# A feature-major residual stream, a second FFN input buffer and a new order of work in a streaming encoder layer on eight cores

## Chip, cores and metric

The kernel runs on the 8 cores of one Trainium2 chip (two dies: cores 0 to 3 and 4 to 7). All cores run the same program, each on its own two prompt sequences (eight tiles of 512 frames) and one sample of 64 frames. The time is the span of the slowest core in microseconds (us). Some executions fall into a slow state, in which a whole die shows a lower granted TensorE clock: of the 12 runs of the changed kernel with cores on record, 8 kept a mean clock of at least 0.96 on every core, and in the other four one die or both showed 0.80 to 0.92. Engines have the profile's names: PE is TensorE, DVE VectorE, ACT ScalarE, POOL GpSimd, SP SyncE. PSUM (tiles named `ps`) holds the sums that PE writes, and L773 is line 773 of that kernel's source.

## The reference

One layer, in JAX, cut to what matters:

```
h = x + 0.5 * swiglu(rms_norm(x, norm_ffn1), w_ffn1_in, w_ffn1_out)          # FFN1
n = rms_norm(h, norm_mix)
q_a,k_a,v_a,r_a,f_a, q_b,k_b,v_b, g_a,g_b = split(n @ w_in)
o_a, s_new = gla_branch(...)         # gated scan, 4 heads, a state passed from chunk to chunk
o_b        = band_attention(...)     # 16 heads, own chunk and the 8 before, learned bias
mixed = sigmoid(g_a) * (o_a @ w_branch_gla) + sigmoid(g_b) * (o_b @ w_branch_att)
h = h + mixed @ w_out                                                        # the "mixer" ends
h = h + 0.5 * swiglu(rms_norm(h, norm_ffn2), w_ffn2_in, w_ffn2_out)          # FFN2
y = rms_norm(h, norm_final)          # d_model 1024, d_ff 2816; keys, values and state are outputs too
```

## The kernel before

The program is a list of operations with priorities, which a scheduler in Python turns into a fixed order per engine. Two streams are woven into each other: F (the FFNs) and M (the mixer: projections, gated scan, attention, merge). In tile i's period, M works on tile i, while F does FFN2 of tile i-1 and FFN1 of tile i+1. FFN matmuls are what TensorE (PE) does while the scan or the attention waits for other engines; I call them filler below.

```
groups = [[tiles[0], make_sample()]] + [[t] for t in tiles[1:]]
P.seg = (-1, "F")
for c in groups[0]: prelude(c)            # load x, norm, transposes into xF
ffn1(0, groups[0])
for i in range(NTILE):
    P.seg = (i, "F")
    if i > 0:
        ffn(i - 1, groups[i - 1], 2)
    if i + 1 < NTILE:
        for c in groups[i + 1]: prelude(c)
        ffn1(i + 1, groups[i + 1])
    P.seg = (i, "M")
    mixer_with_state(i, groups, tiles, mixer)
```

Within a period both streams advance in proportion to their `pace`, which is the PE time of an operation except for attention's score product:

```
P.pe(0.3, qk, r=[qb] + [...], w=[sc], pace=2.2)
```

Weights arrive as fp32. In its first uses a block is cast to bf16 by the load itself, from the POOL queue; then it is stored as bf16, and later uses load that from the SP queue:

```
def wload(cls, blk, i):                   # i: how often the block has been used
    b = P.buf(cls, 4096, "w")
    first = blk % 3
    if i <= first:
        P.load(... in_=wsrc[blk] ..., q="pool")           # fp32 to bf16, 128 x 2048
        if i == first:
            P.store(... out=wsc[blk] ..., q="sp")
    else:
        P.load(... in_=wsc[blk] ...)                      # bf16
```

The residual stream has tokens on the partitions, so each norm sums along the row (DVE, with an accumulator) and transposes the result on PE.

The softmax here doesn't subtract the row's maximum and nothing guards it: scores larger than these inputs give would overflow.

Of the kernel before, what the change touches and what calls it, by code (L numbers as in the profile page):

```python
# [30 lines left out]
    "hF": (5 * 4096, 4096), "hM": (2 * 4096, 4096), "xF": (8192, 8192), "xM": (8192, 8192),  # L31
    "gT": (22 * 1024, 1024), "F": (9 * 1024, 1024), "M": (38 * 1024, 256), "Sb": (8 * 512, 512), "st": (64 * 16, 16),
# [34 lines left out]
class Op:  # L67
    __slots__ = ("eng", "dur", "fn", "deps", "bufs", "wbufs", "dma", "idx", "prio", "seg", "pace", "start", "end", "nwait",
                 "out", "ready", "seq", "sig", "waits", "vc", "dsem", "dval", "sval", "bytes", "nd")


class Program:
# [12 lines left out]
    def op(self, eng, dur, fn, r=(), w=(), dma=False, nbytes=0, pace=None):  # L85
# [38 lines left out]
        o.sig = False  # L124
# [7 lines left out]
    def act(self, n, fn, r=(), w=()):  # L132
        return self.op("act", 0.2 + n * 0.00084, fn, r, w)

    def dve(self, n, fn, r=(), w=()):
        return self.op("dve", 0.11 + n * 0.00105, fn, r, w)

    def pool(self, n, fn, r=(), w=()):
        return self.op("pool", 0.15 + n * 0.0018, fn, r, w)

    def load(self, fn, nbytes, r=(), w=(), q="sp", dur=0.06):
        return self.op(q, dur, fn, r, w, dma=True, nbytes=nbytes)

    def store(self, fn, nbytes, r=(), w=(), q="pool", dur=0.9):
        return self.op(q, dur, fn, r, w, dma=True, nbytes=2 * nbytes)

    def schedule(self, lead):
# [10 lines left out]
        for o in ops:  # L158
            o.out = []
            o.ready = 0.0  # L160
            o.nd = 0
        for o in ops:
            for d, _ in o.deps:
                ops[d].out.append(o.idx)
                o.nd += 1
# [14 lines left out]
        for o in ops:  # L180
            if o.nd == 0:
                avail[o.eng].append((o.prio, o.idx))
        efree = {e: 0.0 for e in ENGINES}
# [3 lines left out]
        ev = [0.0]  # L187
        done = 0
# [38 lines left out]
        while done < nops:  # L227
# [13 lines left out]
            while ev and ev[0] <= tnow + 1e-9:  # L241
                heapq.heappop(ev)
            progress = True
            while progress:
                progress = False
                for e in ENGINES:
# [3 lines left out]
                    for item in avail[e]:  # L250
                        if best is not None and item >= best[0]:
                            continue
                        o = ops[item[1]]
                        if o.ready > tnow + 1e-9:
                            continue
                        spots = []
                        ok = True
                        for b in o.bufs:
                            if id(b) not in placed:
                                p = find(b, tnow)  # L260
                                if p is None:
                                    ok = False
                                    break
                                spots.append((b, p))
# [8 lines left out]
                        best = (item, o, spots)  # L273
                    if best is None:
                        continue
                    item, o, spots = best
                    avail[e].remove(item)
                    for b, p in spots:
# [10 lines left out]
                        unal[b.cls].remove(b)  # L289
                    o.start = tnow  # L290
                    if o.dma:
                        efree[e] = tnow + o.dur
                        s0 = max(tnow + o.dur, bw_free)
                        x = o.bytes / 300e3
                        bw_free = s0 + x
                        o.end = s0 + x + 2.2
# [12 lines left out]
                    for b in o.bufs:  # L309
                        b.users.append(o)  # L310
                        b.left -= 1
                        if b.left == 0:
# [15 lines left out]
                            heapq.heappush(ev, ft)  # L328
                    for d in o.out:
# [6 lines left out]
                        if x.nd == 0:  # L336
                            avail[x.eng].append((x.prio, x.idx))
# [123 lines left out]
def mmt(ncols, n):  # L461
    return n * (max(ncols, 240) * 0.000417 + 0.003)
# [13 lines left out]
]  # L476
LEAD = {"M": 0.04, "F": 0.0}


def build(NSEQ, SEQLEN):  # L480
# [14 lines left out]
    xp = din("xp", [NTOK, D])  # L495
    xsm = din("xs", [64, D])
# [6 lines left out]
    gains_d = din("gains", [128, 4, 8])  # L503
    gnf_d = din("gnf", [1, D])
# [4 lines left out]
    yp = dout("yp", [NTOK, D])  # L509
    ys = dout("ys", [64, D])  # L510
    kpo = dout("kpo", [NSEQ * 512, D])
    vpo = dout("vpo", [NSEQ * 512, D])
    spo = dout("spo", [NSEQ, 4, 128, 256])
    kso = dout("kso", [64, D])
# [4 lines left out]
    h1d = dscr("h1d", [NTOK + 64, D], F32)  # L519
    h2d = dscr("h2d", [NTOK + 64, D], F32)  # L520
# [19 lines left out]
    gains = sb("gains", [128, 4, 8], F32)  # L540
    gnfb = sb("gnfb", [128, D], F32)
# [5 lines left out]
    CMASK = constf[:, 1, :]  # L547

    out_dmas = []
    K = {n: Buf(None, 0, n, base=n) for n in ("kbT", "VB", "Sf", "ident", "constf", "segm", "gains", "gnf", "eps", "cbs",  # L550
# [5 lines left out]
    def init():  # L556
# [3 lines left out]
        P.dve(128, lambda e: e.tensor_copy(out=identb[:], in_=constf[:, 0, :]), r=[K["constf"]], w=[K["ident"]])  # L560
        P.dve(1, lambda e: e.memset(epsb[:], EPS), w=[K["eps"]])

    def init2():
        P.seg = (-0.5, "M")
        P.load(lambda e: e.dma_start(out=wfa[:], in_=wfa_d), 64 << 10, w=[K["wfa"]], q="pool", dur=0.9)
        P.load(lambda e: e.dma_start(out=wgate[0:17, :], in_=wgate_d), 32 << 10, w=[K["wgate"]], q="pool", dur=0.9)
        P.load(lambda e: e.dma_start(out=gnfb[:], in_=gnf_d.partition_broadcast(128)), 512 << 10, w=[K["gnf"]])
# [24 lines left out]
    def wload(cls, blk, i):  # L592
        b = P.buf(cls, 4096, "w")
        first = blk % 3
        if i <= first:
            P.load(lambda e: e.dma_start(out=b.b(), in_=wsrc[blk]), 1 << 20, w=[b], q="pool", dur=0.9)
# [11 lines left out]

    def norm_stat(hb, TP, cls):
        xb = P.buf(cls, 2048, "xb")  # L610
        st = P.buf("st", 16, "st")
        P.dve(1024, lambda e: e.scalar_tensor_tensor(out=xb.b()[:TP, :], in0=hb.f()[:TP, :], scalar=1.0, in1=hb.f()[:TP, :],  # L612
                                                     op0=MUL, op1=MUL, accum_out=st.f()[:TP, 0:1]), r=[hb], w=[xb, st])
        rstd(st, TP, 0, 1, 1.0 / D)
        return xb, st

    def norm_sub(ctx, s, hb, gidx, xdst, strm):
        TP = ctx.TP
        xb, st = norm_stat(hb, TP, strm)
        P.dve(600, lambda e: e.tensor_scalar(out=xb.b()[:TP, :], in0=hb.f()[:TP, :], scalar1=st.f()[:TP, 0:1], scalar2=None,  # L620
                                             op0=MUL), r=[hb, st, xb], w=[xb])
        pb = P.buf("ps" + strm, 2048, "tp")

        def tr(e):
            ins = None
            for k in range(8):
                ins = e.transpose(out=pb.b()[:, k * 128:k * 128 + TP], in_=xb.b()[:TP, k * 128:(k + 1) * 128],
                                  identity=identb[:TP, :TP])
            return ins
        P.pe(0.9, tr, r=[xb, K["ident"]], w=[pb])  # L630

        def ev(e):
            src = pb.b().rearrange("p (k t) -> p k t", k=8)[:, :, 0:TP]
            dst = xdst.b().rearrange("p (k t) -> p k t", k=8)[:, :, s * 128:s * 128 + TP]
            g3 = gains[:, gidx, :].unsqueeze(2).broadcast_to([128, 8, TP])
            return e.tensor_tensor(out=dst, in0=src, in1=g3, op=MUL)  # L636
        P.dve(8 * TP, ev, r=[pb, K["gains"]], w=[(xdst, s)])

    def xk(x, ctx):
        return [(x, s) for s in range(ctx.NS)]  # L640

    def xcols(x, k, ctx):
        return x.b().rearrange("p (k t) -> p k t", k=8)[:, k, 0:ctx.T]

    def xsub(x, k, s, ctx):
        return x.b().rearrange("p (k t) -> p k t", k=8)[:, k, s * 128:s * 128 + ctx.TP]
# [3 lines left out]

    def proj(w, c0, ncol, outs, keys):
        def fn(e):
            ins = None
            for k in range(8):
                for o, x, ctx in outs:
                    ins = e.matmul(o(), lhsT=w3(w, k, c0, ncol), rhs=x(k), start=(k == 0), stop=(k == 7))
            return ins
        dur = sum(mmt(ctx.T, 8) for _, _, ctx in outs)
        return P.pe(dur, fn, r=[w] + keys, w=[])
# [6 lines left out]
    def prelude(ctx):  # L666
        ctx.xF = P.buf("xF" if ctx.NS == 4 else "F", ctx.T * 16, "xF")
        for s in range(ctx.NS):
            pre_sub(ctx, s)

    def pre_sub(ctx, s):
        hb = P.buf("hF", 4096, "h")
        TP = ctx.TP
        P.load(lambda e: e.dma_start(out=hb.f()[:TP, :], in_=ctx.x(s)), TP << 12, w=[hb])
        norm_sub(ctx, s, hb, 0, ctx.xF, "F")

    def ffn(i, ctxs, which):
        wi, wo_ = (W_F1I, W_F1O) if which == 1 else (W_F2I, W_F2O)
        c0 = ctxs[0]
        cs = ctxs[1] if len(ctxs) > 1 else None  # L680
        for c in ctxs:
            c.gT = []
            if c.NS == 1:
                c.gTs = P.buf("F", NJ * 128, "gTs")
        for j in range(NJ):
            ffn_j(i, ctxs, c0, cs, wi + j, j)
        blocks = {}
        for half in range(2):
            acc = {}
            for c in ctxs:  # L690
                for s in range(c.NS):
                    acc[(c, s)] = P.buf("psF" if c is c0 else "psM", 2048, "acc")
            j = 0
            while j < NJ:
                u = half * NJ + j
                n = min(4 - u % 4, NJ - j)
                if u // 4 not in blocks:
                    blocks[u // 4] = wload("ringF", wo_ + u // 4, i)
                for c in ctxs:
                    for s in range(c.NS):  # L700
                        ffn_o(c, s, acc[(c, s)], blocks[u // 4], j, n, u % 4)
                j += n
            for c in ctxs:
                for s in range(c.NS):
                    ffn_e(c, s, acc[(c, s)], half, which)
# [853 lines left out]
```

## Time and profile before

| kernel before | |
|---|---|
| median, all runs of the first session | 4124.12 us (4116.39 to 4605.45) |
| profiled run (fast) | span 4114.9 us |
| PE busy, mean granted clock | 89 %, 0.954 to 0.956 |

### The profile page before, as it was taken

How to read it: one execution, taken by the hardware profiler on the slowest of the kernel's cores; microseconds unless marked ns; L12 is line 12 of the kernel's file. 1: busy time of each engine (PE TensorE's matmuls, PEld its weight loads, DVE VectorE, ACT ScalarE, POOL GpSimd, SP SyncE). 2: the span in 40 equal slices, each digit the busy share in tenths (PEclk: the TensorE clock that was granted, in tenths of full speed). 3: DMA queues.
4: the chain of work that ended last, by engine and by line, in shares of the span. 5: the costliest groups of instructions: out<-in, count | busy, mean ns of one | idle time of the engine just before them, and what ended most of it. 6: DMA issues, size and time to landing. Idle time of an engine off the chain costs nothing.

```text
span 4114.9 us, 60621 instructions; the slowest of 8 cores (4098.3 to 4114.9 us)
## 1 busy us (share of the span) xinstructions
PE 3659.6 (89%) x19384; PEld 1692.0 (41%) x19760; DVE 1755.8 (43%) x2918; ACT 1759.3 (43%) x3324; POOL 392.7 (10%) x795
## 2 busy tenths in 40 slices
PE   3789977897989989999899979999999989999787
PEld 1334433443434434444444434443444434444333
DVE  3245333525435353453425453453425453453333
ACT  2325443524535445254543535254533546254432
POOL 2011111110021101010010000000010000001100
PEclk8999989998999989999899989999999999999799
DMA  9687857775688745755446444634445444644243
GB/s 208 123 185 165 169 121 174 146 155 166 177 217 203 176 166 166 223 171 174 154 146 215 141 160 151 220 132 151 147 153 206 141 159 141 209 150 154 88 153 123
DMA packets 200374, 677.12 MB, mean 165 GB/s; under 512 B 30575, under 2 KB 31232, under 8 KB 200064
## 3 DMA queue, kind: packets, MB, share of 16 engines
q1 hardware_dynamic: 141248, 492.52, 35.7%
q0 software_dynamic: 58816, 180.69, 22.1%
q8 instruction: 166, 2.72, 0.3%
q14 instruction: 144, 1.18, 0.1%
HBM read 668.72 MB, written 121.37 MB: 192 GB/s over the span
## 4 chain that ended last, share of the span: by engine, by line
PE 78%; DVE 6%; issue 5%; ACT 5%; DMA 4%; POOL 0%; ACTq 0%; DVEq 0%; SPq 0%; POOLq 0%
PE ps L726 27%; PE ps L754 14%; PE ps L799 8%; PE ps L1010 6%; PE ps L1228 5%; PE ps L1234 5%; PE ps L1116 3%; PE ps L844 2%; PE ps L1083 2%; PE ps L1260 2%; DMA s_ringM<-w 1%; DMA s_hM<-h1d 1%; ACT s_M L1098 1%; DMA s_ringF<-w 1%; DVE s_F L612 1%
## 5 line engine op out<-in xcount | busy, mean ns | idle before, releaser
L726 PE MATMUL ps<-s_xF,s_ringF 128*128 128x512 bf16 x5466 | 1312.9, 382 | 74.3 <-DVE s_F L740 40.9
L726 PEld LDWEIGHTS ps<-s_xF,s_ringF 128*128 128x128 bf16 x5632 | 538.2, 98 | 743.2 <-issue 166.0
L754 PE MATMUL ps<-s_ringF,s_gT 128*128 128x512 bf16 x2739 | 649.0, 380 | 7.2 <-issue 3.6
L740 DVE TENSOR_TENSOR s_F<-ps,s_F 128x512 f32<-128x512 f32 (+1 forms) x396 | 252.7, 638 | 600.9 <-ACT s_F L664 560.7
L662 ACT ACTIVATE s_F<-ps 128x512 f32<-128x512 f32 (+1 forms) x396 | 219.5, 554 | 650.2 <-PE ps L726 568.6
L1098 ACT ACTIVATE s_M<-ps 128x1024 bf16<-128x1024 f32 (+1 forms) x288 | 286.8, 997 | 411.0 <-DVE ps L1091 362.9
L754 PEld LDWEIGHTS ps<-s_ringF,s_gT 128*128 128x128 bf16 x2816 | 264.0, 98 | 324.8 <-issue 35.8
L799 PE MATMUL ps<-s_ringM,s_xM 128*128 128x512 bf16 x1503 | 351.9, 387 | 13.6 <-DVE s_xM L636 4.8
L1091 DVE TENSOR_TENSOR ps<-ps,s_bias 128x512 f32<-128x512 f32 (+1 forms) x304 | 182.0, 599 | 280.8 <-PE ps L1083 274.5
L1010 PE MATMUL ps<-s_xM,s_ringM 128*128 128x512 bf16 x1001 | 254.5, 405 | 30.9 <-ACT s_M L1098 22.4
L604 ACT ACTIVATE s_st<-s_st,s_epsb 128x1 f32<-128x1 f32 (+2 forms) x168 | 49.2, 293 | 535.6 <-DVE s_F L612 283.4
L741 DVE TENSOR_TENSOR s_gT<-ps,s_F 128x512 bf16<-128x512 f32 x352 | 242.5, 689 | 66.4 <-PE ps L726 45.6
L1243 DVE TENSOR_TENSOR s_M<-ps,s_M 128x512 f32<-128x512 f32 (+1 forms) x144 | 92.0, 639 | 418.0 <-PE ps L1234 233.5
L1228 PE MATMUL ps<-s_xM,s_ringM 128*128 128x512 bf16 x1000 | 242.6, 383 | 16.6 <-ACT s_M L663 9.3
L1234 PE MATMUL ps<-s_M,s_ringM 128*128 128x512 bf16 (+1 forms) x1129 | 246.4, 359 | 3.7 <-DVE s_M L1243 2.3
L663 ACT ACTIVATE s_F<-s_F 128x512 f32<-128x512 f32 (+1 forms) x396 | 232.5, 587 | 28.8 <-ACT s_F L662 0.4
L664 ACT ACTIVATE s_F<-s_F 128x512 f32<-128x512 f32 (+1 forms) x396 | 232.3, 587 | 28.6 <-ACT s_F L663 2.2
L662 ACT ACTIVATE s_M<-ps 128x512 f32<-128x512 f32 (+2 forms) x210 | 118.3, 563 | 284.2 <-PE ps L1228 258.8
L799 PEld LDWEIGHTS ps<-s_ringM,s_xM 128*128 128x128 bf16 x1536 | 148.3, 99 | 194.9 <-issue 35.0
L1116 PE MATMUL ps<-s_M,s_VB 128*128 128x256 bf16 (+3 forms) x888 | 185.7, 324 | 12.0 <-POOL s_M L1104 7.7
L1083 PE MATMUL ps<-s_M,s_kbT 64*128 64x256 bf16 (+3 forms) x896 | 117.3, 317 | 59.0 <-ACT s_M L1098 24.0
L1010 PEld LDWEIGHTS ps<-s_xM,s_ringM 128*128 128x128 bf16 x1024 | 101.3, 103 | 152.7 <-issue 60.9
(150 smaller groups left out, 3587.3 us busy)
## 6 DMA issues: line engine op xcount, KB each, us to landing
s_ringF<-wsc SPq DMA_DIRECT2D x396, 512.0 KB, 3.6
s_ringM<-wsc SPq DMA_DIRECT2D x265, 512.0 KB, 4.1
s_ringF<-w POOLq DMA_DIRECT2D x132, 512.0 KB, 7.0
s_ringM<-w POOLq DMA_DIRECT2D x87, 512.0 KB, 8.0
wsc<-s_ringF SPq DMA_DIRECT2D x66, 512.0 KB, 5.5
s_hF<-xp SPq DMA_DIRECT2D x64, 512.0 KB, 5.4
wsc<-s_ringM SPq DMA_DIRECT2D x44, 512.0 KB, 6.1
s_bias<-btd SPq DMA_DIRECT2D x64, 256.0 KB, 3.0
```

The source lines that it names most:

```text
L662: P.act(n, lambda e: e.activation(out=s.f()[:TP, 0:n], in_=src(), func=AF.Exp, scale=-1.0), r=r, w=[s])
L663: P.act(n, lambda e: e.activation(out=s.f()[:TP, 0:n], in_=s.f()[:TP, 0:n], func=AF.Ln, bias=1.0), r=[s], w=[s])
L726: ins = e.matmul(o(), lhsT=w3(w, k, col, 128), rhs=x(k), start=(k == 0), stop=(k == 7))
L740: P.dve(n, lambda e: e.tensor_tensor(out=s.f()[:, 0:n], in0=g(), in1=s.f()[:, 0:n], op=MUL), r=r1 + [s], w=[s])
L741: P.dve(n, lambda e: e.tensor_tensor(out=gt.b()[:, gk * 64:gk * 64 + n], in0=u(), in1=s.f()[:, 0:n], op=MUL), r=r2 + [s], w=[(gt, gk)])
L754: ins = e.matmul(acc.f()[:TP, :], lhsT=c.gT[j + jj][0].b()[:, c.gT[j + jj][1] * 64 + s * 128:c.gT[j + jj][1] * 64 + s * 128 + TP], rhs=w.b ...
L799: ins = e.matmul(pb.f()[:c.TP, :], lhsT=xsub(x, k, s, c), rhs=ws[k // 4].b()[:, (k % 4) * 512:(k % 4 + 1) * 512], start=(k == 0), stop=(k ...
L1010: ins = e.matmul(pb.f()[:, 0:T], lhsT=w3(w, k, col, 128), rhs=xcols(c.xM, k, c), start=(k == 0), stop=(k == 7))
L1098: return e.activation(out=b, in_=a, func=AF.Exp, scale=0.125)
L1116: ins = e.matmul(acc[hh]()[:, s0 * 128:(s0 + ns) * 128], lhsT=vl(slot(j), 2 * pr + hh), rhs=pp.b()[:, hh * 512 + col:hh * 512 + col + ns * ...
L1228: ins = e.matmul(pg.f()[:, 0:T], lhsT=w3(w, k, 0, 128), rhs=xcols(c.xM, k, c), start=(k == 0), stop=(k == 7))
L1234: ins = e.matmul(px.f()[:, 0:T], lhsT=w3(w, k, 128, 128), rhs=src[k].b()[:, 0:T], start=(k == 0), stop=(k == 7))
```

## The change

Its intent: no norm transposes and fewer other PE operations; FFN work always at hand for the tiles in the middle; an earlier start. The core of the diff (cuts marked):

```
-    "hF": (5 * 4096, 4096), "hM": (2 * 4096, 4096), "xF": (8192, 8192), ...
+    "xF": (2 * 8192, 8192), ...                          # F and M pools grow, hF and hM go
-    xp = din("xp", [NTOK, D])
+    xp = din("xp", [NTILE, 8, 128, 512])                 # features on partitions; so yp, h1d, h2d
...
     def wload(cls, blk, i):
-        first = blk % 3
+        first = blk % 3 if blk >= W_QKB else 1 + blk % 2 # FFN blocks: cast twice or three times
...
+    class Norm:                                          # in place of norm_stat, norm_sub
+        def add(self, h):      # ACT: Square of one chunk; POOL (the last: DVE): add to the sum
+        def rstd(self):        # PE: fp32 all-ones product over the 128 partitions; ACT: Ln, Exp
+    def scaled(...)            # DVE: x * gain * rstd, once per chunk
...
-        for half in range(2): ...                        # FFN out: tokens stationary, 4 sums at once
+        for m in range(8): ffn_m(...)                    # FFN out: weights stationary, 1 sum of 22
-            P.pe(mmt(128, 8 * c.NS), fn, ...)            # separate product for the key output: gone
...
-        P.pe(0.3, qk, ..., pace=2.2)
+        P.pe(0.35, qk, ..., pace=8.0 if c.i in (0, NTILE - 1) else 2.2)
...
+    ffn_in(0, groups[0], 1)                              # prologue: PSUM and weight slots of M borrowed
+    for c in groups[1]: prelude(c)
+    ffn_out(0, groups[0], 1)
     for i in range(NTILE):
         P.seg = (i, "F")
-        if i > 0: ffn(i - 1, groups[i - 1], 2)
-        if i + 1 < NTILE: prelude(...); ffn1(i + 1, ...)
+        if i > 0: ffn_in(i - 1, groups[i - 1], 2)
+        if 0 < i < NTILE - 1: prelude(groups[i + 1])     # before FFN2's output product
+        if i > 0: ffn_out(i - 1, groups[i - 1], 2)
+        if i + 1 < NTILE: ffn_in(i + 1, ..., 1); ffn_out(i + 1, ..., 1)
```

## The prediction

> **What bounds the kernel now.** I read the page first (engine totals, slices), then two windows, then the PE timeline inside them, then the chain of waits of the first 100 us.
>
> ```profile
> PE 3659.6 (89%) x19384; PEld 1692.0 (41%) x19760; DVE 1755.8 (43%) x2918; ACT 1759.3 (43%) x3324; POOL 392.7 (10%) x795
> PE   3789977897989989999899979999999989999787
> PEclk8999989998999989999899989999999999999799
> DMA  9687857775688745755446444634445444644243
> ```
>
> (Page: busy us, share and instructions; then tenths of each fortieth of the span.) PE is the bound; every other engine is under half busy. But PE dips in the first three slices, in slices 6 and 7, in the last three and once per tile, and the granted clock dips with it. The two windows show a dip beside a dense stretch:
>
> ```profile
> 930.00:985.00 55.00, 31.21 (x149) 13.03 (x151) 35.75 (x50) 18.28 (x35) 5.49 (x14) 0.66 0.58 177
> 1000.00:1200.00 200.00, 198.55 (x977) 88.38 (x996) 68.30 (x107) 103.64 (x155) 27.47 (x54) 1.00 0.73 184
> ```
>
> (Second number: length; then PE busy.) In the dense stretch PE is busy 198.55 of 200 us at clock 1.00; in the dip 31 of 55 at 0.66. The timeline says why:
>
> ```profile
> 973.92 1.01 PE L627 MATMUL ps<-s_identb,s_F 128*128 128x128 bf16 x8 [1.23 <-DVE s_F L620]
> 979.39 1.01 PE L627 MATMUL ps<-s_identb,s_F 128*128 128x128 bf16 x8 [3.07 <-DVE s_F L620]
> ...
> 1043.72 0.39 PE L1083 MATMUL ps<-s_M,s_kbT 64*128 64x512 bf16 x2
> 1044.04 3.63 PE L726 MATMUL ps<-s_xF,s_ringF 128*128 128x512 bf16 x16
> ```
>
> L1083 is an attention score product, which must be followed by bias, exp and mask elsewhere. Dense stretches fill that wait with 3.6 us of FFN matmuls (L726). In the dip the FFN stream has nothing: FFN2 has ended, and the next tile's norm and transposes (L627) must write the one input buffer before FFN1 can start. Attention stands bare. The FFN stream is without matmuls from 936 to 985, 1456 to 1494, 1946 to 1978, 2410 to 2443, 2863 to 2902 and 3330 to 3368 us. The start is a different fault:
>
> ```profile
> 21.23 42.90 DMA s_ringM<-w
> 64.67 22.41 DMA s_ringF<-w
> ```
>
> [...]mixer weights, caches and bias stores stand ahead of the FFN's fifth weight block, so PE waits until 87.7 us.
>
> [...]16 attention projections at N=512 take 3.45 us at 1034.3 in the chain, so 216 ns[...]8 such matmuls take 3.44 us at 550.4, double[...]
>
> **The floor and the loss.** I counted every matmul in each built program[...] the 512 and 64 wide ones, 216 and 29 ns in the timeline[...]. Before: 19,760 matmuls, 14,776 of them 512 wide, sum 3524 us. Span 4115, so 591 us are lost. Cut at the first forget-gate product (L813) of each tile, which start at 258, 698, 1233, 1722, 2211, 2660, 3128 and 3592 us, the nine stages last 258, 439, 536, 489, 490, 449, 467, 464, 523 against floors of 139, 337, 451, 441, 447, 412, 431, 431, 434. Lost: 119, 102, 85, 48, 42, 37, 36, 33, 89.
>
> **The change part by part.**
>
> ```profile
> L627 PE MATMUL ps<-s_identb,s_F 128*128 128x128 bf16 (+1 forms) x528 | 49.6, 252 | 104.4 <-DVE s_F L620 103.8 <-DVE s_gT L741 0.4
> L1034 PE MATMUL ps<-s_ringM,s_xM 128*128 128x128 bf16 x512 | 31.2, 219 | 0.0
> L612 DVE SCALAR_TENSOR_TENSOR s_F<-s_hF 128x1024 bf16<-128x1024 f32 (+1 forms) x99 | 119.6, 1220 | 16.8 <-DMA s_hF<-xp 14.6
> L663 ACT ACTIVATE s_F<-s_F 128x512 f32<-128x512 f32 (+1 forms) x396 | 232.5, 587 | 28.8 <-ACT s_F L662 0.4
> L1217 POOL TENSOR_TENSOR s_M<-s_M 128x512 bf16<-128x512 f32 x72 | 83.4, 1158 | 617.6 <-DVE s_M L1243 617.5
> ```
>
> (Busy, mean ns, idle before.) 1. The residual stream lies feature-major. All 792 norm transposes go: 768 x 56 + 24 x 29 ns = 44 us of floor. The key output reuses the projection (L1034 goes): 512 x 56 + 64 x 56 = 32 us. FFN-out and out-projection swap operands: the same 512-wide count for prompts; the sample's 104 wide matmuls become 416 narrow: -22 + 12 = -10 us. Added: 36 FP32 all-ones products for the norm sums, 32 x 4 x 216 ns + 4 small = 28 us. Net -58 us: the built program gives 3466. By stages: 137, 324, 453, 435, 430, 412, 430, 430, 417.
>
> 2. Other engines. DVE loses the statistics, scaling and transposed evictions (L612 160 us in both streams, its accumulator reads 11, L620 74, L636 117, L781 42: 404) and gains 256 scalings and 50 adds of about 0.67 us plus small ones, some 215: near 1570. ACT gains 256 squares at 0.587 and 64 Ln/Exp at 0.587 (188, with the sample 197) and loses 132 rstd pairs at 0.293 + 0.202 (65): near 1890. POOL gains 174 adds at 1.16 and 24 small ones (208) and some 150 DMA issues at 0.53 (80): near 680. At 3690 us these are 43, 51 and 18%: none becomes the bound, so this is all off the path except in norm tails.
>
> 3. Order. A second FFN input buffer, and the prelude of the next tile placed before FFN2's output product. In the new PE order FFN-in follows FFN-out directly and every score product of the middle tiles has FFN work behind it. So the FFN stream's gap closes: in the 55 us window above, PE was idle 24. I count 24 in each of six tiles, 144 us.
>
> 4. Residual tiles out of the general buffers instead of two. Now out-projection waits for a store to free its buffer, then a load: at 1679 the chain has 9.0 + 6.0 us of DMA. I count some 12 us (one such wait, part of it covered) at each of six tile boundaries, 72 us.
>
> 5. Start: PSUM and weight slots of the idle mixer stream are borrowed, caches come later, 16 weight blocks stand together at the head of POOL's queue, FFN1 blocks aren't stored in tile 0. First FFN matmul: x at about 18 us as now (transposes start at 18.2), then square, add, FP32 product, Ln, Exp and paced scalings, some 6 + 4: 28 us lost. Then 22 blocks at 3.9 us (now 6 us each from 100 to 195 us, one in flight). I allow 10 for DMA and 7 for the tail: loss 45 instead of 119.
>
> 6. First and last tile: attention's pace is raised from 2.2 to 8, so FFN work is spread under it. Losses 102 to 35 and 89 to 55 (bare attention at 3800-3900 goes; the last FFN2's 16 us tail and 10 us head stay). For the tiles between, parts 3 and 4 make 216 us of 85 + 196; I book 201, since gap and boundary partly overlap: the second tile, which keeps three PSUM banks per step while the sample runs (waits of 1.8 us on L740 at 743), goes from 85 to 35, the other five from 196 to 45.
>
> Sum: 3466 + 45 + 35 + 35 + 45 + 55 = 3681; I say 3690.
>
> **Rivals.** A: DMA takes over early. Cast loads rise from 219 to 252. The queue table gives queue 1 492.5 MB in 35.7% of the span, 335 GB/s, so 1.56 us for a bf16 block; queue 0 has 22.1%, 909 us, of which its 65 MB of stores take 195 at that rate, and 219 cast blocks the other 714: 3.26 us each. Estimate: the first 175 us need 33 cast FFN blocks, some 6 for the mixer and 13 MB besides, 127 + 39 = 166 us; tile 0, some 360 us long, needs 69 cast blocks (225), 31 block stores (49) and 17 MB (51), 325 us. For it: share 0.85 already now over 0 to 258 us. Against: it reaches 1.1 to 1.2 under backlog between 25 and 100 us. It would add 40 to 80: 3730 to 3770. B: the norm's chain (ACT, POOL, PE, ACT, DVE) becomes the new wait at tile ends. Against: the order puts 5 to 12 us of FFN matmuls behind each of its products. If they don't cover it, 8 us (six steps of 0.6 to 0.9 and the paced scalings) at 16 ends, 128 us: 3810. C: only the floor moves, because bare attention is bound by its own exp chain: 4115 - 58 = 4057. Against: the dense stretches at clock 1.00 with the same attention.[...]
>
> **Range and chances.** The floor is firm to 10 us; the loss of 215 could be 150 (all dips closed) or 330 (A or B): 3616 to 3796, so 3620 to 3800. Faster by over 2% needs under 4042[...]. 0.96 / 0.03 / 0.01.
>
> **What would show it.** Mean clock near 0.98, PE busy near 95%, the per-tile dips gone from the slices, first FFN matmul by 30 us and first forget-gate product near 180; ACT near 1890, DVE near 1570, POOL near 680. FP32 products near 0.9 us each. Wrong if early slices keep 7s with PE waiting on weight DMA (A), if PE's waits name the norm's DVE scalings (B), or if dips stay with FFN matmuls available (C).

## More of the kernel before

For what follows I cut the span into nine stages, at the first forget-gate product (512 columns) of each tile. The stage before tile 0 is the start; the last one holds tile 7's mixer and its FFN2. Three of these stages of the kernel before, as windows (from:to, length, then busy us and count of PE, weight load, DVE, ACT and POOL, granted clock, DMA share, GB/s):

```profile
258.00:698.00 440.00, 370.59 (x2321) 179.07 (x2363) 191.22 (x370) 190.74 (x438) 67.26 (x122) 0.93 0.74 157
2660.00:3128.00 468.00, 442.52 (x2197) 200.97 (x2239) 210.88 (x337) 213.27 (x382) 29.05 (x68) 0.97 0.47 160
3592.00:4115.00 523.00, 457.95 (x2345) 208.43 (x2388) 202.27 (x322) 215.93 (x376) 39.89 (x84) 0.93 0.41 136
```

PE stands still for 69, 25 and 65 us in these three. The first and the last stage are the poor ones, and only one FFN call runs beside the mixer in each.

## The result, and the profile after

| | before | after |
|---|---|---|
| median of all runs | 4129.20 us (17 runs) | 3865.28 us (11 runs) |
| lowest run | 4116.39 us | 3854.78 us |
| ratio of fast runs | | 0.9368 (95 % interval 0.9353 to 0.9382) |

A ratio is the mean time of one kernel's fast runs over that of the other's fast runs of the same rounds, so it is not quite the ratio of these medians. Executions in which one die ran at a lower clock are left out of the means. The direction was right and the time was not: 3690 us and a range of 3620 to 3800 us were predicted.

The page of the changed kernel (fast run, span 3866.4 us): engine totals, then fortieths of the span in tenths.

```profile
PE 3589.8 (93%) x18776; PEld 1619.7 (42%) x18776; DVE 1595.9 (41%) x2784; ACT 1903.3 (49%) x3420; POOL 696.7 (18%) x1143
PE   5878888989989999999999999999999999988988
PEclk9988999999999999999999999999999999989999
DMA  7896699777898956777474555545464545533454
```

The middle of the span is now solid nines. What is left are the lower digits at the left (all of slices 1 to 7, two more up to slice 12) and at the right (four of the last five), just where the kernel before was poor as well. The stages as windows:

```profile
0.00:219.00 219.00, 149.23 (x1090) 73.45 (x1090) 84.60 (x190) 80.67 (x186) 49.39 (x96) 0.95 0.82 161
219.00:652.00 433.00, 367.61 (x2254) 171.38 (x2253) 160.45 (x332) 199.27 (x439) 101.88 (x171) 0.92 0.79 161
2481.00:2915.00 434.00, 431.98 (x2149) 193.88 (x2148) 189.61 (x313) 231.66 (x390) 65.61 (x104) 1.00 0.52 173
3349.00:3866.00 517.00, 446.77 (x2090) 192.34 (x2090) 188.93 (x309) 228.75 (x378) 67.15 (x114) 0.93 0.41 140
```

In the third, a middle tile, PE is busy 432 of 434 us at a granted clock of 1.00. In tile 0 (second) and the last stage (fourth) it still stands 65 and 70 us, and the clock is lower there (0.92 and 0.93). DMA is busy in tile 0 (0.79) and calm in the last stage (0.41), so the two need not have the same cause.

Cut in the same way on all eight cores, with the median of the cores in each stage (us). The floor is an estimate, the prediction's count of matmuls, and "predicted" its floor plus its loss. The time for each matmul agrees with the spacing of starts in the trace of the kernel before: 216 ns at 512 columns (16 take 3.45 us at 1034.3), 56 ns at 128 (32 of L1034 from 1852.99 us) and 29 ns at 64 (16 of L1010 from 445.45 us).

| stage | before | floor | predicted | after | after minus predicted |
|---|---|---|---|---|---|
| start | 257 | 137 | 182 | 209 | +27 |
| tile 0 | 436 | 324 | 359 | 431 | +72 |
| tile 1 | 537 | 453 | 488 | 509 | +21 |
| tiles 2 to 6 | 2354 | 2137 | 2182 | 2181 | -1 |
| tile 7 and end | 522 | 417 | 472 | 516 | +44 |

The median core takes 3842 us; the slowest, which sets the time, 24 us more in the profiled run. So the sum over the middle tiles is right to a microsecond, and the whole miss lies in the first three stages and the last. The agreement of that sum is in part luck: the prediction spread 45 us of loss over five tiles, and they lost 15, 13, 7, 4 and 5.

### The profile page after: what moved, and what is told of

Same layout as the page of the kernel before. It is cut to its first block, busy times and chain, and to the rows that moved or that the text cites. A ratio compares the mean times of both kernels' runs of the same rounds, so it can differ in the third digit from the quotient of the medians.

```text
span 3866.4 us, 60436 instructions; the slowest of 8 cores (3822.3 to 3866.4 us)
## 1 busy us (share of the span) xinstructions
PE 3589.8 (93%) x18776; PEld 1619.7 (42%) x18776; DVE 1595.9 (41%) x2784; ACT 1903.3 (49%) x3420; POOL 696.7 (18%) x1143
## 3 DMA queue, kind: packets, MB, share of 16 engines
q0 software_dynamic: 65632, 198.00, 26.2%
## 4 chain that ended last, share of the span: by engine, by line
PE 79%; DMA 9%; DVE 4%; ACT 4%; issue 3%; POOL 1%; SPq 0%; DVEq 0%; ACTq 0%; POOLq 0%
PE ps L773 28%; PE ps L803 14%; PE ps L831 8%; PE ps L1042 5%; PE ps L1249 5%; PE ps L1255 5%; PE ps L876 3%; PE ps L1137 3%; PE ps L1291 2%; DMA s_ringM<-w 2%; PE ps L1104 2%; DMA s_M<-xs 1%; DMA s_F<-xp 1%; ACT s_M L1119 1%; DMA s_ringF<-w 1%
## 5 line engine op out<-in xcount | busy, mean ns | idle before, releaser
L773 PE MATMUL ps<-s_xF,s_ringF 128*128 128x512 bf16 x5456 | 1298.9, 384 | 34.7 <-DVE s_xF L661 15.5
L773 PEld LDWEIGHTS ps<-s_xF,s_ringF 128*128 128x128 bf16 x5456 | 521.9, 99 | 674.1 <-issue 124.3
L803 PE MATMUL ps<-s_gT,s_ringF 128*128 128x512 bf16 x2736 | 643.2, 381 | 8.3 <-DMA s_ringF<-w 5.0
L1119 ACT ACTIVATE s_M<-ps 128x1024 bf16<-128x1024 f32 (+1 forms) x288 | 286.4, 994 | 310.1 <-DVE ps L1112 276.3
L803 PEld LDWEIGHTS ps<-s_gT,s_ringF 128*128 128x128 bf16 x2736 | 262.4, 98 | 333.7 <-issue 38.7
L640 ACT ACTIVATE s_F<-s_F 128x512 f32<-128x512 f32 x192 | 119.0, 627 | 282.6 <-DVE s_F L817 217.7
L1249 PE MATMUL ps<-s_xM,s_ringM 128*128 128x512 bf16 x1024 | 243.5, 381 | 4.8 <-DVE s_M L1090 2.1
L1042 PE MATMUL ps<-s_xM,s_ringM 128*128 128x512 bf16 x1024 | 235.3, 381 | 8.2 <-ACT s_M L1119 6.8
L646 POOL TENSOR_TENSOR s_F<-s_F 128x512 f32<-128x512 f32 x126 | 160.0, 1270 | 323.8 <-ACT s_F L640 308.3
L1137 PE MATMUL ps<-s_M,s_VB 128*128 128x256 bf16 (+3 forms) x896 | 173.7, 306 | 7.8 <-POOL s_M L1125 4.5
L817 DVE SCALAR_TENSOR_TENSOR s_F<-ps,s_F 128x512 f32<-128x512 f32 x128 | 87.8, 689 | 173.5 <-PE ps L803 142.8
```

Of the source, the lines that this page charges most:

```text
L773: ins = e.matmul(o(), lhsT=w3(w, k, col, 128), rhs=x(k), start=(k == 0), stop=(k == 7))
L803: ins = e.matmul(acc[c].f()[:, 0:c.T], lhsT=w.b()[:, (u + jj - j) * 128:(u + jj - j + 1) * 128], rhs=g.b()[:, k * 64:k * 64 + c.T], start= ...
L1042: ins = e.matmul(pb.f()[:, 0:T], lhsT=w3(w, k, col, 128), rhs=xcols(c.xM, k, c), start=(k == 0), stop=(k == 7))
L1119: return e.activation(out=b, in_=a, func=AF.Exp, scale=0.125)
L1137: ins = e.matmul(acc[hh]()[:, s0 * 128:(s0 + ns) * 128], lhsT=vl(slot(j), 2 * pr + hh), rhs=pp.b()[:, hh * 512 + col:hh * 512 + col + ns * ...
L1249: ins = e.matmul(pg.f()[:, 0:T], lhsT=w3(w, k, 0, 128), rhs=xcols(c.xM, k, c), start=(k == 0), stop=(k == 7))
```

## The experiments

Theories after the result. Theory A (rival A of the prediction): early casting loads and stores of weights hold the start, tile 0 and tile 1. Theory F (of filler): filler is a fixed stock. Beside tile 0's mixer there is only FFN1 of tile 1, beside tile 7's only FFN2 of tile 6, so raising attention's pace merely takes filler from the scan. Unless said otherwise, each run is the changed kernel with one edit, results are correct, the numbers are means of fast runs (the changed kernel: 3864.3 us), and stages are medians of the eight cores in one profiled run. A ratio stands for the time over that of the kernel before, with its 95 % interval; the changed kernel has 0.9368. Python lays out the order of work anew for each edit, so an edit can also move other operations.

### 1. The pace put back

```
-  pace=8.0 if c.i in (0, NTILE - 1) else 2.2
+  pace=2.2
```

> The changed kernel with the pace of attention in the first and last tile put back from 8 to 2.2, nothing else. Theory F (filler is a fixed stock: in these two tiles only one FFN call runs beside the mixer, so spreading it only decides whether the gated scan or the attention stands bare): time within 1 % of the changed kernel, 3827 to 3904 us, loss of the last stage still 85 to 110 us, but the scan dense and the attention bare. Rival P (the prediction's step: the pace is what covers attention): the last stage and tile 0 lose 60 to 100 us more, 3930 to 3970 us.

Measured: 3863.5 us (ratio 0.9374, 0.9345 to 0.9403): the same. Tile 0 took 445 us rather than 431, the last stage 512 rather than 516. What PE waited for in the mixer of the last tile (wait, total us, times, longest), the changed kernel and then this one:

```profile
PE ps L1104 <- ACT s_M L1119: 16.9, 15, 2.4
PE ps L1009 <- POOL s_Sb L999: 8.8, 10, 1.5
```

```profile
PE ps L1104 <- ACT s_M L1119: 22.7, 21, 3.3
PE ps L1009 <- POOL s_Sb L999: 4.2, 6, 1.1
```

L1104 is the score product, which waits for PSUM that the exp (ACT, L1119) still reads; L1009 is the scan's product with the state, which waits for the state's copy (POOL, L999). With the low pace attention waits 5.8 us more and the scan 4.6 us less: 26.9 against 25.7 in sum. The pace moves the wait from one to the other. These two are 26 of the 70 us in which PE stands in that stage; the rest is spread over many shorter waits. My expectation of a dense scan and a quite bare attention was too strong, but the step that the prediction gave 101 us is worth 14 in tile 0 (one profiled run each) and nothing in the last stage, and the total doesn't show it.

### 2. No casts

```
-  if i <= first: load fp32, casting, POOL queue; if i == first: store bf16
-  else: load bf16
+  load bf16 (host hands over the upper halves of the fp32 words; for measurement only)
```

> Weights handed over as bf16 (the upper halves of the fp32 words, only for measurement): no casting loads, no weight stores, half the bytes of the early loads. Rival A (DMA and its casting bind the start and tile 0): start and tile 0 lose 60 to 110 us less, 3755 to 3805 us. Theory F (DMA is at 0.6 to 0.7 in tile 0 while PE waits for scan and exp): the start gains 10 to 25 us, tile 0 under 15 and tile 1 under 15, so 3815 to 3850 us.

Measured: 3769.3 us (ratio 0.9145, 0.9124 to 0.9166): 95 us less. Start 185, tile 0 397, tile 1 493, tile 2 435 (from 450), the last stage 521. That is rival A's number, not mine: tile 0 gives back 33 us where I allowed 15. PE's longest waits for weight blocks in tile 0 of the changed kernel come to 14.5 us of it (from 260 to 650 us):

```profile
PE ps L1291 <- DMA s_ringM<-w: 8.2, 2, 6.0
PE ps L803 <- DMA s_ringF<-w: 3.6, 4, 2.0
PE ps L773 <- DMA s_ringF<-w: 2.7, 2, 1.9
```

The start is then 3 us and tile 1 5 us from the prediction. Tile 0 keeps 38 us too much with a DMA that is busy 0.42 of the time, as its window in this run shows, and the last stage is no shorter:

```profile
186.00:584.00 398.00, 348.25 (x2188) 165.68 (x2228) 159.20 (x336) 194.97 (x433) 58.21 (x88) 0.94 0.42 133
```

So both theories hold, each for a part.

### 3. The all-ones product in bf16

```
-  last addition writes fp32; matmul(ss, lhsT=ONES fp32, rhs=a.f())
+  last addition writes bf16; matmul(ss, lhsT=ONES bf16, rhs=ab.b())
```

> The all-ones product of the norm in bf16 (the last addition writes bf16), nothing else. The trace gives one 512-wide fp32 product two instructions of 592 ns, so 32 of them take 38 us of PE against 7 in bf16. Theory (they lie on PE's path in dense stretches): 24 to 32 us less, 3833 to 3841 us. Rival (they lie in waits of PE that are there anyway): under 10 us less, 3855 us or more. If a product cost 864 ns as the prediction had it: 21 us less.

Measured: 3858.3 us (ratio 0.9361, 0.9332 to 0.9390): not told from the changed kernel. My expectation misread the trace. An fp32 product is two instructions of 592 ns, but they overlap. The timeline of the changed kernel inside a dense stretch shows it:

```profile
2892.45 1.02 PE L652 MATMUL ps<-s_M,s_constf 128*128 128x512 f32 x2
2893.31 2.97 PE L803 MATMUL ps<-s_gT,s_ringF 128*128 128x512 bf16 x13
```

From the start of the pair to the next matmul are 0.86 us, as the prediction had it (4 x 216 ns). The 21 us that bf16 should still save in all don't appear: the middle stages stay at 434 us. In the window of one middle tile PE's wait for the norm's scaling (L661, here L666) is 3.7 us in place of 1.9, which would be rival B in small. Otherwise it is open where they went: the interval of 0.3 % is too wide for it, and the scheduler laid out many other operations in another order too.

### 4. All of x ahead of the sample

```
+  prologue: load all eight prompt chunks first, then square and add   # changed kernel: 7 chunks, sample, 1 chunk
```

> In the prologue all eight prompt chunks are loaded before the sample's, so the eighth chunk no longer stands behind eight slow sample loads (issued at 23 us now). Theory Q (queue order holds the first norm): first FFN matmul from 47 us to 38 to 42, 5 to 9 us less in all, about 3858 us. Rival V (volume: five weight blocks of 1 MB and x share the DMA, and the sample is needed too by the first FFN product): first FFN matmul stays at 45 to 48 us, time same within 3 us.

Measured: 3869.6 us (ratio 0.9381, 0.9348 to 0.9414), first FFN matmul still at 48 us, as rival V had it. The order of x and sample is not what holds the start; experiment 11 takes up the volume.

### 5. FFN work put off into the last tile

```
   period 6:  - FFN2(5) in, prelude, out; FFN1(7) in, out
              + FFN1(7) in, out; FFN2(5) in            # its prelude one period earlier
   period 7:  + FFN2(5) out                            # 38 us of matmuls, then FFN2(6) as before
```

> FFN work moved: in the last tile but one, FFN1 of the last tile goes first, and the output product of the FFN2 before it (38 us) is put off into the last tile. Nothing added or removed. Theory F (the last tile's mixer lacks filler, one FFN call of 114 us in place of two): the last stage's loss falls by 15 to 25 us and little comes back in the stage before, 3838 to 3852 us. Rival (the last stage's loss is the tail and the chains themselves): 3858 to 3870 us.

Measured: 3843.3 us (ratio 0.9329, 0.9290 to 0.9368). Period 6 shrank by 44 us (435 to 391), the last stage grew by 15 (516 to 531): 38 us of matmuls cost the last stage 15. This is theory F's number, and the first gain that needs nothing but another order. The intervals of the two ratios still touch; it is the stages that carry the reading.

### 6. More filler in the last tile

```
+  if i == NTILE - 1: ffn_in(i - 1, groups[i - 1], 2)    # computed twice, the first copy dropped
```

> In the last tile the first half of its FFN call (352 matmuls 512 wide, 76 us of PE floor) is computed twice; the first copy is thrown away, the result is right. Theory F: 30 to 45 of the 76 us fall into waits, so 31 to 46 us more, 3894 to 3909 us, and the scan and attention stretch shows fewer waits. Rival (waits do not take filler): 70 to 80 us more, 3933 to 3943 us.

Measured: 3888.5 us (ratio 0.9439, 0.9418 to 0.9459): 24 us more for 76 us of matmuls, 5 us below the range that I gave. The last stage grew by 28, so 48 us of its 99 us of loss took filler. What PE waited for longest in that stage:

```profile
PE ps L773 <- DVE s_xF L661: 4.4, 1, 4.4
PE ps L1009 <- POOL s_Sb L999: 4.4, 5, 2.0
```

The 16.9 us of the score product are gone from the list; what leads is one wait for a norm's scaling (L661) and a half of the scan's wait.

### 7 and 14. The order of the middle tiles undone

Experiment 7 takes the second buffer away and puts the next tile's prelude behind FFN2's output product again. Experiment 14 does the latter alone.

```
-  ffn_in(i - 1, 2); prelude(i + 1); ffn_out(i - 1, 2)
+  ffn_in(i - 1, 2); ffn_out(i - 1, 2); prelude(i + 1)
-  "xF": (2 * 8192, 8192)                                # 7 only
+  "xF": (8192, 8192)
```

> One FFN input buffer again, and the next tile's prelude after FFN2's output product; the rest of the change stays. The prediction's part 3 booked 24 us for each of six tiles: 120 to 150 us more, 3983 to 4013 us, dips of the PE slices back once per tile. Rival (the dips were the old norm with its transposes rather than the buffer): 20 to 60 us more, 3883 to 3923 us.

> Two FFN input buffers stay, but the next tile's prelude stands after FFN2's output product again. If the place of the prelude closes the dips: nearly the full effect of the one-buffer run comes back, 3960 to 4000 us. If the second buffer does it (the scheduler can hoist the prelude once it has a buffer): 3862 to 3890 us.

Measured: 4000.3 us (7) and 3996.5 us (14; ratio 0.9689, 0.9633 to 0.9745). Both lose 132 to 136 us, nearly all of it in tiles 1 to 6: 18, 24, 22, 18, 26 and 26 us per stage in experiment 14. The page of 14 has its dips back, once per tile:

```profile
PE   5888898997989899998999989998999989988988
```

The prediction booked 24 us for each of six tiles, 144 us. It holds, and the cause is the place of the prelude: the second buffer without it brings nothing (4000 us without, 3997 with). Whether the early prelude would also do with one buffer was not tried.

### 8. Casts in thirds again

```
-  first = blk % 3 if blk >= W_QKB else 1 + blk % 2
+  first = blk % 3                                       # 219 casting loads for 252
```

> The FFN's weight blocks are cast on their first one, two or three uses in thirds as in the kernel before (219 casting loads in place of 252; a third of them is stored at its first use). Casting loads as the cost, 3.26 us each by the prediction's estimate, of which half is saved: tile 0 and tile 1 shrink by 15 to 30 us together and the start grows by up to 10: 3845 to 3860 us. Rival (the order of stores matters as much, or only the start's volume): 3860 to 3880 us.

Measured: 3859.2 us (ratio 0.9368, 0.9346 to 0.9389): no difference. Start and tile 0 grew by 4 us each (more stores fall there), tiles 1 and 2 shrank by 12 and 7; the last stage, which casts nothing, happened to take 6 more. The total is in the range that I gave, but tile 0 went the other way. So the 33 added casts, on which rival A was built, cost nothing net that these runs could tell (some 9 us). That the stores which they put off give back what they take is my reading of the stages.

### 9 and 10. Stores and casts taken apart

Experiment 9 keeps the casting loads and drops the stores (later loads read the host's bf16 copy). Experiment 10 keeps stores and queues, and only lets the 252 loads read bf16 in place of fp32.

```
9:  -  if i == first: store wsc[blk]       else: load wsc[blk]
    +                                      else: load wbf[blk]
10: -  wsrc = din("w", [NBLK, 128, 2048])
    +  wsrc = din("w", [NBLK, 128, 2048], BF16)          # same POOL queue, same places
```

> Half of what the run without casts took away: casting loads stay as they are, but no weight block is stored; later loads come from a bf16 copy handed over by the host (measurement only). If the stores (110 of 0.5 MB) carry the DMA cost: 3800 to 3830 us. If the casting loads do: 3845 to 3862 us.

> The other half: the 252 casting loads read bf16 from the host's copy, from the same POOL queue in the same places, and the stores stay. If the bytes and conversion of casting are the cost: 3775 to 3815 us. If it is the place in POOL's queue (loads behind additions and waits), the time stays near 3850 to 3865 us, since the queue is unchanged.

Measured: 3830.5 us (9; ratio 0.9295, 0.9280 to 0.9309) and 3805.2 us (10; ratio 0.9233, 0.9203 to 0.9264). So the stores cost 34 us and the casting 59, in sum 93 of the 95 of experiment 2. The place in POOL's queue, which 10 leaves as it is, is left with 2 us, though the interval of 10 alone is 13 us to either side. Two things stay joined: a load that casts reads fp32, so it reads twice the bytes as well (HBM reads of 685.5 MB, against 553.4 in experiment 10), and without the store (9) later loads no longer wait for one. The queue tables (packets, MB, share of 16 engines' span) of the changed kernel and of experiment 10:

```profile
q1 hardware_dynamic: 159120, 474.71, 37.1%
q0 software_dynamic: 65632, 198.00, 26.2%
```

```profile
q1 hardware_dynamic: 159120, 474.71, 37.9%
q0 software_dynamic: 65632, 198.00, 16.1%
```

Queue 0 writes the same 198 MB in both, yet takes 26.2 % of 3866 us (1013 us) with casting and 16.1 % of 3795 (611 us) without. That is 402 us for 252 blocks, 1.6 us of all 16 engines per block. The prediction's estimates, 3.26 us for a cast block and 1.56 for a bf16 one, differ by 1.7, which agrees; only the weight that it gave them was too small.

### 11. Weight blocks after x

```
+  prologue: blocks 2 to 8 of FFN1 wait for the last prompt chunk; chunks are all loaded before they are squared
+  the sample in one load with rows of 2 KB, in place of eight with rows of 256 B
```

> In the prologue the weight blocks after the first wait for the last prompt chunk of x, and the sample comes in one load with 2 KB rows rather than eight with 256 B rows. Theory V (five casting blocks and x share the DMA): first FFN matmul from 47 to 30 to 38 us; of these 9 to 17 us a part comes back as waits on the blocks, time 3848 to 3862 us. Rival (the volume of the whole start counts, not its order): first FFN matmul earlier, but time 3860 to 3870 us.

Measured: 3849.9 us (ratio 0.9342, 0.9325 to 0.9358); start 195 us. The chain of waits of the start (start us, length, what), the changed kernel and then this one:

```profile
12.75 16.68 DMA s_M<-xs
...
37.93 2.06 PE ps L652 x2
...
47.54 22.66 PE ps L773 x161
```

```profile
18.71 2.06 PE ps L666 x2
...
31.70 18.39 PE ps L802 x131
```

The prompt's norm product (L652, here L666) moves from 38 to 19 us and the first FFN matmul (L773, here L802) from 48 to 32, near the 28 of the prediction. Of these 16 us, 14 arrive at the end of the stage. The edit has two new parts (experiment 4's order, which it contains, brought nothing alone), and which of them counts more is not told apart.

### 12, 15, 16, 17. Candidates

12 joins experiments 11, 5 and 8. 15 joins 11 and 5, casts FFN1 as in the changed kernel and FFN2 in thirds, and has pace 4 in the last tile. 16 is 15 with pace 8. 17 is 16 with 8 of 22 column groups of FFN2(5)'s first product moved into the last tile as well.

```
15, 16, 17:  +  first = blk % 3 if blk >= W_F2I else 1 + blk % 2
15:          +  pace=8.0 if c.i == 0 else 4.0 if c.i == NTILE - 1 else 2.2
17:          +  period 6: ffn_in(5, 2, range(14)); period 7: ffn_in(5, 2, range(14, 22)); ffn_out(5, 2)
```

> A candidate for a better kernel: the later weight blocks of the last run, the FFN work put off into the last tile, and casts in thirds. Sum of the single effects: 3825 to 3848 us.

> Candidate: late weight blocks in the prologue, FFN work put off into the last tile, pace 8 in tile 0 and 4 in the last, casts in thirds for FFN2 and the mixer only. Stage by stage from the single runs: start 195, tile 0 433, tile 1 503, tile 2 441, the rest as in the deferral run: 3795 to 3815 us.

> The candidate before with pace 8 in both tiles: start 194, tile 0 431, tile 1 510, tile 2 442, the last stage 531 to 534 in place of 540: 3805 to 3822 us.

> As the candidate beside it, and eight of the 22 column groups of that FFN-in product (28 us) move from the last tile but one into the last tile. Theory F: the stage they leave shrinks by 26 to 30 us, the last grows by 10 to 20: 8 to 18 us less than the candidate beside it. If the last stage is full by now: the same within 4 us.

| | mean us | ratio (95 % interval) |
|---|---|---|
| 12 | 3819.1 | 0.9267 (0.9225 to 0.9309) |
| 15 | 3828.4 | 0.9283 (0.9239 to 0.9326) |
| 16 | 3821.9 | 0.9272 (0.9253 to 0.9291) |
| 17 | 3827.8 | 0.9299 (0.9240 to 0.9358) |

Experiments 12, 15 and 16 beat both kernels: about 1 % below the changed one (for 16, 0.9272 / 0.9368 = 0.990). 12 came out 6 us below its expectation and 15 missed its own by 13 us: with pace 4 its last stage took 540 us, not 531 as in experiment 5. But 16, with pace 8, took 536, so the pace is 4 of these 9 us at most. 17 is not settled: period 6 shrank by 18 us and the last stage grew by 12 against 16, three of its runs lie at 3808 to 3823 us, and a fourth, counted as fast, at 3865, with one die at a clock of 0.964 to 0.969 and the other at 0.978 to 0.983.

### 13. More filler in tile 0, without casts

```
   as experiment 2, and
+  if i == 0: ffn_in(1, groups[1], 1)                    # computed twice, the first copy dropped
```

> As the run without casts (3768 us, tile 0 397 us), and in tile 0 the FFN-in product of the next tile is computed twice (352 matmuls, 76 us of PE floor, the first copy thrown away; 22 more block loads). Theory F (tile 0 lacks filler like the last tile, where 48 of 76 us were absorbed): tile 0 grows by 28 to 48 us, time 3796 to 3816 us. Rival (tile 0's remaining 73 us is DMA or the sample's own chain and takes no filler): tile 0 grows by 65 to 80 us, 3833 to 3848 us.

Measured: 3813.2 us (ratio 0.9246, 0.9226 to 0.9266): 44 us more than experiment 2 for 76 us of matmuls. The total is in theory F's range, but tile 0 grew by 54, between that theory (28 to 48) and its rival (65 to 80), and tile 1 shrank by 7. What PE waited for in tile 0 in experiment 2 and here (L1100 is the score product, L1005 the scan's; the lines are shifted by four):

```profile
PE ps L1100 <- ACT s_M L1115: 11.0, 6, 2.6
PE ps L1005 <- POOL s_Sb L995: 6.6, 8, 1.4
```

```profile
PE ps L1005 <- POOL s_Sb L995: 2.4, 3, 0.9
...
PE ps L1100 <- ACT s_M L1115: 2.1, 1, 2.1
```

The two waits fall from 17.6 to 4.5 us; a new one of 6.7 us, for a norm's scaling, heads the list instead. So 22 us of the 73 that tile 0 still lost without casts took filler, 32 if tile 1's gain is counted in. That these lie within the 38 us by which tile 0 missed the prediction is my reading; the remainder is open.

## Why the prediction was right and wrong

By its own parts:

- Part 1, the floor: right. The middle stages lie within 5 us of their floors where DMA is calm (434 against 430 twice; share 0.52 in the stage from 2481 us), and an fp32 product takes 0.86 us at 512 columns. No run had shown the latter when it was predicted, for the kernel before has no such product.
- Part 2, engines: right, and off the path. DVE 1596 (1570 predicted), ACT 1903 (1890), POOL 697 (680).
- Part 3, order: right. 144 us predicted, 132 us when undone. Only the place of the prelude is needed to explain it.
- Part 4, residual tiles: too large, as far as can be argued. Tiles 2 to 6 fell by 173 us: 25 are floor (2162 to 2137), 116 came with the prelude (experiment 14, 24 + 22 + 18 + 26 + 26), so 32 stay for everything else, not 12 us at each of five boundaries. It was hidden, since the prediction booked less than the sum of parts 3 and 4, so that the sum came out right partly by luck. No run tested part 4 alone.
- Part 5, start: the step "First FFN matmul: x at about 18 us as now" failed. The norm product waits for x and starts at 37.93 us; the 10 us from there to the first FFN matmul are as predicted. In the median core that matmul comes at 47 us, not 28, which is 19 of the 27 us of the miss; what follows lost 25 us, not 17 ("I allow 10 for DMA and 7 for the tail"). Without casts (2) the two are 36 and 12, so the stage's 185 us against 182 are two errors that cancel. With the blocks after x (11) they are 31 and 26. The 18 us were misread already in the kernel before: 18.2 is the start of its first transposes, and the last ones start 13 us later:

```profile
18.21 1.89 PE L627 MATMUL ps<-s_identb,s_F 128*128 128x128 bf16 x16 [18.21 <-DVE s_F L620]
30.86 1.54 PE L627 MATMUL ps<-s_identb,s_F 128*128 128x128 bf16 x16 [4.50 <-DVE s_F L620]
35.20 0.59 PE L726 MATMUL ps<-s_xF,s_ringF 128*128 128x512 bf16 x1 [2.79 <-DVE s_M L587]
```

- Part 6, first and last tile: failed in its mechanism, "attention's pace is raised from 2.2 to 8, so FFN work is spread under it. Losses 102 to 35 and 89 to 55". The losses by the table are 107 and 99. There is one FFN call to spread, and spreading doesn't add to it (experiment 1); adding filler does shrink the loss (5, 6, 13). Casts and stores are another 33 of tile 0's 107 (2). The kernel before had already shown it: its windows of these two stages have PE standing 69 and 65 us.

Of the rivals, A was right in mechanism. The prediction gave it 40 to 80 us on top of its 3690; it was 95. The argument against it, that the DMA share rises above 1 under backlog (1.14 from 25 to 100 us in the kernel before), doesn't bear: tile 0 stood at 0.79 on average and still got 33 us faster without casts. That single blocks come late although the average has room is my reading; PE's waits for weight blocks there, 8.2 + 3.6 + 2.7 us, show a part of it. Its trigger was wrong as well, for the 33 added casts make no difference that the runs could tell (experiment 8). B can be dropped for the middle: in the stage from 2481 to 2915 us PE stood only 2 us. C describes the first and last tile, but the waits there yield to filler, so the exp chain is not the bound for the 48 and 22 us that did.

In numbers, for the median core: of the 161 us between 3842 and the predicted sum of 3681, casts and stores account for 83 (3842 to 3759), and lack of filler, as experiments 6 and 13 let one read, for most of the 38 and 44 us that tile 0 and the last stage keep. The slowest core lies 24 us above the median one with casts and 6 without (3765 against 3759) in the profiled runs, 12 to 24 and 6 to 10 over all fast runs, so a part of this belongs to the early DMA too.

The doubled time of the eight matmuls at 550.4 us (3.44 us, against 1.73 at 216 ns each) falls in a window of low clock: from 543.4 to 553.4 us the kernel before has a granted clock of 0.50. The longest time that PE stood idle is 2.34 us in that window and 1.65 us in the 7 us before it. How the clock follows from idle time is not shown by this.

## What to carry to other kernels

Before you book a gain from spreading work under waits, count how much work is there to spread in that very stage; a schedule moves filler, it doesn't make any. Test a gain in the stages where the mechanism lacks its material (first and last tile) apart from the middle, where the sum held. And weigh a rival by what it removes when taken away whole: the casts were common to both kernels, so comparing their number before and after hid their price.
